# A hybrid decoder trunk: recurrent chains of two head pairs run side by side, and the output projection's order of contraction

## The chip, the cores and the metric

One core of one Trainium2 chip. The metric is the time of one execution on the device, in microseconds, as the median of several runs. Of one execution there is also a hardware trace. TensorE multiplies matrices (its weight loads are traced apart), VectorE, ScalarE and GpSimd (POOL) do the elementwise work, and SyncE (SP) issues the DMAs.

## The reference, cut to what matters

Two residual layers over 512 tokens of width 1024. Layer 0 mixes tokens by sparse attention, layer 1 by a recurrence (RWKV-7). Both add a cross-attention into 256 memory tokens, project the concatenated heads and end with a SwiGLU FFN. The recurrence of layer 1 has 12 heads of width 64; per head, step by step:

```python
def step(state, inp):
    r_t, w_t, k_t, v_t, a_t, b_t = inp
    sa = jnp.einsum('bhvk,bhk->bhv', state, a_t)
    state = state * w_t[:, :, None, :] + sa[..., None] * b_t[:, :, None, :] \
        + v_t[..., None] * k_t[:, :, None, :]
    return state, jnp.einsum('bhvk,bhk->bhv', state, r_t)
...
y = ((y - mean) * lax.rsqrt(var + GN_EPS)).reshape(B, S, MIX_WIDTH)
y = y * lnx_w.astype(jnp.float32) + lnx_b.astype(jnp.float32)
out = (y + bonus.reshape(B, S, MIX_WIDTH)) * g.astype(jnp.float32)
...
x = x + jnp.concatenate([mix, cross], axis=-1) @ w_o[i]
x = x + _swiglu(_rmsnorm(x, norm2[i]), w_ffn_in[i], w_ffn_out[i])
```

## The kernel before

All activations lie with features on the 128 partitions and the 512 tokens along the row. Large products are made of 128x128x512 matmuls of float32 operands that are split into a high and a low part, three matmuls for each (`mm3`, L686; `gemm`, L692; weights are loaded by `wraw`, L667, and split by ScalarE and VectorE in `wsplit`, L672).

The program is first recorded as a list of operations (`Rec`), and then a planner (`schedule`, L317) makes the order of each engine from estimated costs: the ready operation with the lowest number goes first. It may run ahead of the oldest operation not yet issued by a number of operations that depends on the kind (`LOOK`, L541: 600 for most, 1650 for the projections marked as filler), as far as buffers allow (84 shared row buffers `s2`, 8 PSUM banks, a share of both held back) and weights up to a quota (`QUOTA`, L520: 14 buffers, 24 in the phase named "ffn"). On TensorE it prefers an operation of the tile size that is running, within a limit of numbers (`TILED`, L528). What it lays down is fixed; on the chip each engine works through its list in order.

Layer 1 (`rwkv`, L1237): the projections of r, k and v by `gemm`, then for each of 6 pairs of heads `rwkv_pair` (L1336). It prepares decay, gates and keys with small low-rank products, among them the five matmuls of the gate, whose result ScalarE copies to the tile `dgt`. `rwkv_unit` (L1448) then turns the recurrence into 8 chunks of 64 tokens: matrices within a chunk (tiles `ar`, `bk`, `gram`, `tm`, and five levels of a triangular inverse in `tT`, `tQ`), all by 64x64 matmuls, one for each of the two heads, that sit in different corners of TensorE. This part is called the unit below. Its last loop is the chain: for every chunk, a right-hand side from the state (ScalarE copies it to `pad`), the solution u (copied by ScalarE again), the new state (VectorE, with a scaled old state from POOL), and an output of the chunk (`py`, copied to `ry`). After the chain the output is normalized, transposed (`gyo`), the bonus added and multiplied by the gate into `ot`. Pair m+1 follows pair m in the list, so the planner lays the unit of the next pair, and projections, between the steps of a chain. Every matmul of float32 operands of width 64 shows as two records in the trace.

The output projection (`out_proj`, L895) splits the eight tiles `ot` (`oxh`, `oxl`; 0 to 5 are mixer heads, 6 and 7 the memory's) and makes eight `gemm`s over all eight tiles in order, each with its bank, then adds the residual. In layer 0, heads come in four groups of three, and the compressed branch (`otc`) is added to tiles 0 to 5 after the last group.

Of the kernel before, what the change touches and what calls it, by code (L numbers as in the profile page):

```python
# [19 lines left out]
S = 512  # L20
# [218 lines left out]
class Rec:  # L239
# [16 lines left out]
    def add(self, eng, meth, args, kw, alts=()):  # L256
# [12 lines left out]
        if after is not None:  # L269
            dep(after, 0)  # L270
# [270 lines left out]
LOOK = {"far": 1650, "all": 600, "sync": 300, "w": 3000}  # L541
# [75 lines left out]
class B:  # L617
# [277 lines left out]
    def out_proj(self, i, ot, back):  # L895

        nc = self.nc
        xs = [self.split(ot[k], "ox") for k in range(KT)]
        xt = []
        for m in range(8):  # L900
            x = self.s2("xt")
            nc.sync.dma_start(x, back[m])
            ps = self.gemm(self.a[f"w_o{i}"][m], xs)
            nc.vector.tensor_tensor(out=x, in0=ps, in1=x, op=ALU.add)
            xt.append(x)
        return xt
# [37 lines left out]
    def nsa(self, xt):  # L944
# [215 lines left out]
        for g in range(G):  # L1160
# [15 lines left out]
            for qt in range(4):  # L1176
# [60 lines left out]
    def rwkv(self, xt):  # L1237
# [83 lines left out]
        pads = [self.s2("pad", F32, (128, 6, 64)) for _ in range(2)]  # L1321
        pad = [[t[:, j] for j in range(6)] for t in pads]
        for m in range(6):
            r, v = pair(m, m, "rr", 12 + m, 12 + m, "rv_")
            if m == RW_MEM[0]:
                kv = self.mem_kv(1)
            if m == RW_MEM[1]:
                qm = pair(21, None, "qm", 22, None, "qm")
            for j in range(2):
                if m == RW_MEM[2 + j]:  # L1330
                    ot[6 + j] = self.s2("ot")
                    self.mem_attn(j, qm[j], kv, ot)
            ot[m] = self.rwkv_pair(m, r, ks[m], v, rns, selT, zs, dv, pad[m % 2])
        return ot

    def rwkv_pair(self, m, r, k, v, rns, selT, zs, dv, pad):  # L1336
# [58 lines left out]
        wend = self.sm("wend", [128, 8], bufs=3)  # L1395
# [14 lines left out]
        Sp, Rp, Up = [pad[0], pad[1]], [pad[2], pad[3]], [pad[4], pad[5]]  # L1410
        nc.gpsimd.memset(Sp[0], 0.0)
        y = self.s2("ry")
        self.uev = None
        self.rwkv_unit(c3(r), c3(wc), c3(iw), c3(kn), c3(ka), c3(kp), vf, wend, Sp, Rp, Up, y)

        y3 = c3(y)
        mu = self.sm("gmu", [128, 8])
        nc.vector.tensor_reduce(out=mu, in_=y3, op=ALU.add, axis=AX.X)
        nc.vector.tensor_scalar(out=mu, in0=mu, scalar1=1.0 / 64, scalar2=None, op0=ALU.mult)
        tt(out=y3, in0=y3, in1=mu[:, :, None].to_broadcast([128, 8, 64]), op=ALU.subtract)  # L1420
        sq = self.s2("gsq")
        nc.scalar.activation(sq, y, AF.Square)
        var = self.sm("gvar", [128, 8])
        nc.vector.tensor_reduce(out=var, in_=c3(sq), op=ALU.add, axis=AX.X)
        nc.vector.tensor_scalar(out=var, in0=var, scalar1=1.0 / 64, scalar2=64e-5, op0=ALU.mult,
                                op1=ALU.add)
        rs = self.rsqrt(var, [128, 8], "gn")
        tt(out=y3, in0=y3, in1=rs[:, :, None].to_broadcast([128, 8, 64]), op=ALU.mult)

        yo = self.s2("gyo")  # L1430
        yo4 = yo.rearrange("p (b j t) -> p b j t", b=4, j=2)
        pt = self.ax_ps()
        for b in range(4):
            nc.tensor.transpose(pt[:, b * 128:b * 128 + 128], y[:, b * 128:b * 128 + 128],
                                self.ident)
        p4 = pt.rearrange("p (b i t) -> p b i t", b=4, i=2)
        for i in range(2):
            hs = slice(64 * i, 64 * i + 64)
            for j in range(2):
                nc.scalar.activation(yo4[hs, :, j, :], p4[64 * j:64 * j + 64, :, i, :],  # L1440
                                     AF.Identity, bias=self.v("lnb", m)[hs],
                                     scale=self.v("lnw", m)[hs])
        tt(out=yo, in0=yo, in1=bon, op=ALU.add)
        o = self.s2("ot")
        tt(out=o, in0=gt, in1=yo, op=ALU.mult)
        return o

    def rwkv_unit(self, r3, wc3, iw3, kn3, ka3, kp3, vf, wend, Sp, Rp, Up, y):  # L1448
# [107 lines left out]
        nc.scalar.copy(tfin, ps)  # L1556

        for cc in range(8):
            c = cc % 4
            ar, LR, MR = ars[cc // 4], LRB[cc // 4], MRK[cc // 4]  # L1560
            st, s_new = Sp[cc % 2], Sp[(cc + 1) % 2]
            rh, u = Rp[cc % 2], Up[cc % 2]
            vc = vf[:, cc]
            ps = self.ax_ps()[:, 0:64]
            both(ps, MR[:, c, 0], vc, True, False, after=self.uev)
            both(ps, ar[:, c, 0], st, False, True)
            rev = nc.scalar.copy(rh, ps)
            ps = self.ax_ps()[:, 0:64]
            both(ps, tfin[:, cc], rh, True, True)
            self.uev = nc.scalar.copy(u, ps)  # L1570
            if cc < 7:
                sw = self.sm("sw", [128, 64], bufs=3)
                wl = wend[:, cc:cc + 1]
                nc.gpsimd.tensor_scalar(out=sw, in0=st, scalar1=wl, scalar2=1.0,
                                        op0=ALU.mult, op1=ALU.mult)
                ps = self.ax_ps()[:, 0:64]
                both(ps, ktm[:, cc], vc, True, False, after=rev)
                both(ps, btm[:, cc], u, False, True)
                nc.vector.scalar_tensor_tensor(out=s_new, in0=ps, scalar=wl, in1=sw,
                                               op0=ALU.mult, op1=ALU.add)  # L1580
            ps = self.ax_ps("py")[:, 0:64]
            both(ps, ar[:, c, 1], st, True, False, after=rev)
            both(ps, MR[:, c, 1], vc, False, False)
            both(ps, LR[:, c, 1], u, False, True)
            nc.scalar.copy(y[:, cc * 64:cc * 64 + 64], ps)
# [177 lines left out]
```

## Time and profile before

| | us |
|---|---|
| median of 3 runs | 1470.31 |
| lowest, highest | 1467.98, 1472.65 |
| the profiled execution | 1467.86 |
| its span, first to last instruction | 1466.0 |
| TensorE busy | 1434.5 (98%) |
| VectorE busy | 870.5 (59%) |
| ScalarE busy | 689.5 (47%) |
| POOL busy | 121.8 (8%) |

A matmul's end in the trace is modelled, and matmuls overlap; what one costs is read from start to start. The trace has the stages in this order: layer 0's attention up to about 287 us, its output projection up to 335, the FFN up to 691, layer 1's first projections up to 763, the recurrence up to 1060, its output projection up to 1094, and the second FFN with the final norm.

### The profile page before, as it was taken

To read this page: it belongs to the slowest core of one execution; us is meant where nothing else is said; L and a number is where in the kernel's file an instruction comes from. 1 tells how busy PE (TensorE), PEld (TensorE's weight loads), DVE (VectorE), ACT (ScalarE), POOL (GpSimd) and SP (SyncE) were. 2 spreads that over 40 slices of the span, in tenths; PEclk is the share of its full clock that TensorE was granted. 3 is DMA by queue.
4 is the path that set the end of the run, shared out by engine and by line. 5 is a ranking of instruction groups with operands and counts; after the bars stand their busy time and mean duration, and the time that the engine had idled before them with its cause. 6 is when DMAs were issued, how large, how long until landed. Compare 5 with 4: busy or idle time off the path is not lost.

```text
span 1466.0 us, 25256 instructions
## 1 busy us (share of the span) xinstructions
PE 1434.5 (98%) x9914; PEld 1154.3 (79%) x9914; DVE 870.5 (59%) x1806; ACT 689.5 (47%) x1570; POOL 121.8 (8%) x217
## 2 busy tenths in 40 slices
PE   9999999999999999999999999998999999999997
PEld 7977777788888888888777777776678888888886
DVE  7785589974444534455569586787274444434435
ACT  7674578753313432233555575686363322312314
POOL 0231024300000000000000110120000000000003
PEclk9999999999999999999999999998999999999999
DMA  7324423142233322333221201101232332332212
GB/s 250 121 70 128 124 65 110 57 133 84 86 115 101 129 93 94 101 115 106 87 86 52 67 23 39 45 16 45 79 123 83 103 115 88 101 101 86 83 58 77
DMA packets 50232, 133.42 MB, mean 91 GB/s; under 512 B 6208, under 2 KB 14784, under 8 KB 50112
## 3 DMA queue, kind: packets, MB, share of 16 engines
q1 hardware_dynamic: 50112, 131.80, 28.4%
q8 instruction: 78, 1.28, 0.4%
q14 instruction: 42, 0.34, 0.1%
HBM read 122.34 MB, written 4.19 MB: 86 GB/s over the span
## 4 chain that ended last, share of the span: by engine, by line
PE 87%; DVE 6%; ACT 4%; issue 1%; DMA 1%; POOL 1%; SPq 0%; ACTq 0%; DVEq 0%; POOLq 0%
PE pm L516 68%; PE pa L516 13%; PE pv L516 2%; PE ptr L516 1%; PE po L516 1%; PE py L516 1%; ACT gyo L516 1%; POOL p L516 1%; ACT p L516 1%; DVE ot L516 1%; DVE gram L516 1%; DVE wsp L516 0%; DVE p L516 0%; DVE apl L516 0%; DMA kl<-kl 0%
## 5 line engine op out<-in xcount | busy, mean ns | idle before, releaser
L516 PE MATMUL pm<-fxh,wsp 128*128 128x512 f32 x1408 | 434.8, 389 | 0.0
L516 DVE TENSOR_TENSOR wsp<-wraw,wsp 128x512 fp32r<-128x512 f32 (+2 forms) x432 | 279.2, 659 | 51.3 <-ACT wsp L516 50.7
L516 PEld LDWEIGHTS pm<-fxh,wsp 128*128 128x128 f32 x1408 | 264.3, 188 | 55.0
L516 ACT CAST wsp<-wraw 128x512 fp32r<-128x512 f32 (+2 forms) x432 | 238.8, 592 | 96.8 <-DMA wraw<-w_fi 63.6
L516 PE MATMUL pm<-fxl,wsp 128*128 128x512 f32 x704 | 274.2, 389 | 0.0
L516 PE MATMUL pm<-hxh,wsp 128*128 128x512 f32 (+1 forms) x736 | 220.4, 380 | 0.0
L516 PEld LDWEIGHTS pm<-hxh,wsp 128*128 128x128 f32 x736 | 136.3, 188 | 26.3
L516 PEld LDWEIGHTS pm<-fxl,wsp 128*128 128x128 f32 x704 | 132.1, 188 | 27.2
L516 PE MATMUL pm<-hxl,wsp 128*128 128x512 f32 (+1 forms) x368 | 139.5, 380 | 0.0
L516 PE MATMUL pm<-wxh,wsp 128*128 128x512 f32 x368 | 130.7, 415 | 0.0
L516 DVE TENSOR_TENSOR xt<-pm,xt 128x512 f32<-128x512 f32 (+1 forms) x80 | 50.3, 636 | 130.5 <-PE pm L516 130.4
L516 ACT CAST hxh<-hu 128x512 fp32r<-128x512 f32 x44 | 27.3, 620 | 208.7 <-DVE hu L516 208.7
L516 DVE TENSOR_TENSOR hu<-pm,R 128x512 f32<-128x512 f32 x44 | 30.4, 692 | 120.7 <-PE pm L516 120.7
L516 ACT ACTIVATE hg<-hg 128x512 f32<-128x512 f32 x44 | 27.8, 632 | 153.2 <-DVE hg L516 153.2
L516 PE MATMUL pm<-oxh,wsp 128*128 128x512 f32 x256 | 86.3, 406 | 1.6 <-DVE wsp L516 0.7
L516 PE MATMUL pm<-nxh,wsp 128*128 128x512 f32 x256 | 86.3, 400 | 0.8 <-ACT nxh L516 0.8
L516 PEld LDWEIGHTS pm<-wxh,wsp 128*128 128x128 f32 x368 | 67.6, 188 | 19.1 <-issue 5.6
L516 PEld LDWEIGHTS pm<-hxl,wsp 128*128 128x128 f32 x368 | 69.2, 188 | 13.1
L516 DVE TENSOR_TENSOR hg<-pm,R 128x512 f32<-128x512 f32 x44 | 30.4, 691 | 79.6 <-PE pm L516 74.5
L516 POOL TENSOR_SCALAR p<-p,ars,gate 128x128 f32<-128x128 f32 (+3 forms) x96 | 63.1, 671 | 169.4 <-DVE ars L516 84.2
L516 PE MATMUL pm<-wxl,wsp 128*128 128x512 f32 x184 | 75.5, 410 | 0.0
L516 ACT ACTIVATE p<-p,amn 128x128 f32<-128x128 f32 (+3 forms) x96 | 53.4, 559 | 12.0 <-DVE amn L516 11.7
(317 smaller groups left out, 2284.1 us busy)
## 6 DMA issues: line engine op xcount, KB each, us to landing
wraw<-w_fi SPq DMA_DIRECT2D x88, 512.0 KB, 3.4
wraw<-w_fo SPq DMA_DIRECT2D x24, 512.0 KB, 3.4
wraw<-w_rw SPq DMA_DIRECT2D x23, 512.0 KB, 3.5
wraw<-w_fo SPq DMA_DIRECT2D x24, 384.0 KB, 3.0
wraw<-w_o SPq DMA_DIRECT2D x16, 512.0 KB, 3.5
wraw<-w_nsa SPq DMA_DIRECT2D x12, 512.0 KB, 3.8
xt<-xT SPq DMA_DIRECT2D x16, 256.0 KB, 3.8
bias<-bias SPq DMA_DIRECT2D x12, 256.0 KB, 3.9
```

The source lines that it names most:

```text
L516: o.ret = getattr(getattr(nc, o.eng), o.meth)(*[res(x) for x in o.args], **{k: res(v) for k, v in o.kw.items()})
```

## The change

The recurrence's chains are taken out of `rwkv_unit`. For each of three groups, two pairs are prepared (each with its unit), and then `rwkv_chain` runs both chains step by step: the matmuls of both pairs for one sum go to one PSUM bank, 64 columns each, and one ScalarE copy of 128 columns takes both. The state update is still one VectorE and one POOL operation for each pair. `rwkv_out` normalizes the outputs in two blocks of four chunks for both pairs, and makes the gate products only there, after the last u of the chain; the multiplication reads them from PSUM. `out_proj` goes through the eight output tiles in two halves of four: for each half first the contraction over the tiles 0 to 3, 6 and 7, then over 4 and 5; four banks are held meanwhile. It runs in the phase "ffn". In layer 0, `otc` is added to tiles 0 to 3 after the third group and to 4 and 5 after the fourth. The lookahead for most operations goes from 600 to 900, and the first part of the memory attention of layer 1 comes one pair earlier.

```diff
...
-LOOK = {"far": 1650, "all": 600, "sync": 300, "w": 3000}
+LOOK = {"far": 1650, "all": 900, "sync": 300, "w": 3000}
...
-    def out_proj(self, i, ot, back):
...
+    def out_proj(self, i, ot, back, late):
+        nc = self.nc
+        early = [k for k in range(KT) if k not in late]
+        xs = {k: self.split(ot[k], "ox") for k in early}
         xt = []
+        for m0, n in zip((0, MO[0]), MO):
+            ps, ws = [], []
+            for ks in (early, late):
+                for j in range(n):
+                    if ks is early:
+                        x = self.s2("xt")
+                        nc.sync.dma_start(x, back[m0 + j])
+                        xt.append(x)
+                        ws.append(self.wload(self.a[f"w_o{i}"][m0 + j]))
+                        ps.append(self.mm_ps())
+                    for k in ks:
+                        if k not in xs:
+                            xs[k] = self.split(ot[k], "ox")
+                        wh, wl = ws[j][k // 4]
+                        w = slice(k % 4 * 128, k % 4 * 128 + 128)
+                        self.mm3(ps[j], wh[:, w], wl[:, w], *xs[k], k == early[0], k == late[-1])
+                    if ks is late:
+                        x = xt[m0 + j]
+                        nc.vector.tensor_tensor(out=x, in0=ps[j], in1=x, op=ALU.add)
         return xt
...
+            for m in {2: (0, 1, 2, 3), 3: (4, 5)}.get(g, ()):
+                nc.vector.tensor_tensor(out=ot[m], in0=ot[m], in1=otc[m], op=ALU.add)
...
-        for m in range(6):
-            nc.vector.tensor_tensor(out=ot[m], in0=ot[m], in1=otc[m], op=ALU.add)
...
-            ot[m] = self.rwkv_pair(m, r, ks[m], v, rns, selT, zs, dv, pad[m % 2])
+        for g in range(3):
+            pairs = []
+            for m in (2 * g, 2 * g + 1):
+                r, v = pair(m, m, "rr", 12 + m, 12 + m, "rv_")
+                if m == RW_MEM[0]:
+                    kv = self.mem_kv(1)
+                if m == RW_MEM[1]:
+                    qm = pair(21, None, "qm", 22, None, "qm")
+                for j in range(2):
+                    if m == RW_MEM[2 + j]:
+                        ot[6 + j] = self.s2("ot")
+                        self.mem_attn(j, qm[j], kv, ot)
+                pairs.append(self.rwkv_pair(m, r, ks[m], v, rns, selT, zs, dv))
+            ys = self.rwkv_chain(pairs)
+            ot[2 * g], ot[2 * g + 1] = self.rwkv_out(2 * g, pairs, ys, zs)
...
-        ps = self.ax_ps()
-        self.mm3(ps, wh[:, 256:384], wl[:, 256:384], zgh, zgl, True, False)
-        nc.tensor.matmul(ps, wh[:, 384:512], z32, start=False, stop=False)
-        nc.tensor.matmul(ps, wl[:, 384:512], z32, start=False, stop=True)
-        gt = self.s2("dgt")
-        nc.scalar.copy(gt, ps)
...
+    def rwkv_out(self, m0, pairs, ys, zs):
...
+        for j in range(2):
+            wh, wl = pairs[j]["wg"]
+            tt(out=yos[j], in0=yos[j], in1=pairs[j]["bon"], op=ALU.add)
+            ps = self.ax_ps("pg")
+            nc.tensor.matmul(ps, wh[:, 256:384], zgh, start=True, stop=False, after=self.uev)
+            nc.tensor.matmul(ps, wh[:, 256:384], zgl, start=False, stop=False)
+            nc.tensor.matmul(ps, wl[:, 256:384], zgh, start=False, stop=False)
+            nc.tensor.matmul(ps, wh[:, 384:512], z32, start=False, stop=False)
+            nc.tensor.matmul(ps, wl[:, 384:512], z32, start=False, stop=True)
+            o = self.s2("ot")
+            tt(out=o, in0=ps, in1=yos[j], op=ALU.mult)
+            out.append(o)
+        return out
...
+    def rwkv_chain(self, pairs):
+        nc = self.nc
+        heads = [slice(64 * i, 64 * i + 64) for i in range(2)]
+        def sums(name, *terms, after=None):
+            ps = self.ax_ps(name)[:, 0:128].rearrange("p (j d) -> p j d", j=2)
+            first = [None, None]
+            for n, (w, x) in enumerate(terms):
+                for j in range(2):
+                    for i, hs in enumerate(heads):
+                        o = nc.tensor.matmul(ps[hs, j], w(j)[hs], x(j)[hs],
+                                             start=n == 0 and j == 0, stop=n == len(terms) - 1,
+                                             tile_position=(64 * i, 64 * i), skip_group_check=True,
+                                             after=[first[i]] if first[i] else
+                                             [after] if after else None)
+                        first[i] = first[i] or o
+            return ps
+        S = self.sm("cS", [128, 2, 64], bufs=3)
+        nc.gpsimd.memset(S, 0.0)
+        ys = [self.s2("ry", F32, (128, 4, 2, 64)) for _ in range(2)]
+        uev = None
         for cc in range(8):
+            q, c = cc // 4, cc % 4
+            al = lambda j: pairs[j]["ars"][q][:, c, 0]
+            rho = lambda j: pairs[j]["ars"][q][:, c, 1]
+            rbt = lambda j: pairs[j]["LRB"][q][:, c, 1]
+            mt = lambda j: pairs[j]["MRK"][q][:, c, 0]
+            rkt = lambda j: pairs[j]["MRK"][q][:, c, 1]
+            tf, bt, kt, v = (lambda j, n=n: pairs[j][n][:, cc] for n in ("tfin", "btm", "ktm", "vt"))
+            st = lambda j, S=S: S[:, j]
+            ps = sums("pa", (mt, v), (al, st), after=uev)
+            rh, u = self.sm("crh", [128, 2, 64], bufs=2), self.sm("cu", [128, 2, 64], bufs=2)
             rev = nc.scalar.copy(rh, ps)
+            ps = sums("pa", (tf, lambda j: rh[:, j]))
+            uev = nc.scalar.copy(u, ps)
+            ut = lambda j: u[:, j]
             if cc < 7:
+                sw = self.sm("sw", [128, 2, 64], bufs=2)
+                for j in range(2):
+                    nc.gpsimd.tensor_scalar(out=sw[:, j], in0=S[:, j],
+                                            scalar1=pairs[j]["wend"][:, cc:cc + 1], scalar2=1.0,
+                                            op0=ALU.mult, op1=ALU.mult)
+                ps = sums("pa", (kt, v), (bt, ut), after=rev)
+                S = self.sm("cS", [128, 2, 64], bufs=3)
+                for j in range(2):
+                    nc.vector.scalar_tensor_tensor(out=S[:, j], in0=ps[:, j],
+                                                   scalar=pairs[j]["wend"][:, cc:cc + 1],
+                                                   in1=sw[:, j], op0=ALU.mult, op1=ALU.add)
+            ps = sums("py", (rho, st), (rkt, v), (rbt, ut), after=rev)
+            nc.scalar.copy(ys[q][:, c], ps)
+        self.uev = uev
+        return ys
...
-            xt = self.out_proj(i, ot, back)
+            nc.phase = "ffn"
+            xt = self.out_proj(i, ot, back, [[4, 5], [4, 5]][i])
...
-RW_MEM = [0, 4, 5, 5]
+RW_MEM = [0, 4, 4, 5]
+MO = [4, 4]
```

## Rows read from the trace of the kernel before

**Rows 1.** Page, part 1: busy us, share of the span, instructions of each engine.
```profile
PE 1434.5 (98%) x9914; PEld 1154.3 (79%) x9914; DVE 870.5 (59%) x1806; ACT 689.5 (47%) x1570; POOL 121.8 (8%) x217
```

**Rows 2.** Stretches: from:to us, engines' busy us (instructions), granted clock, DMA share, GB/s.
```profile
335.00:691.00 356.00, 356.00 (x1573) 294.77 (x1572) 169.58 (x279) 113.34 (x209) 2.35 (x6) 1.00 0.32 102
...
763.00:1023.00 260.00, 250.95 (x3992) 185.72 (x3991) 200.21 (x443) 173.36 (x439) 32.42 (x62) 0.98 0.15 46
1023.00:1060.00 37.00, 37.00 (x458) 24.02 (x457) 10.26 (x21) 10.82 (x35) 2.28 (x6) 0.96 0.21 73
```

**Rows 3.** Timeline, TensorE, one chunk of the last chain: start us, us, instruction.
```profile
1038.30 0.33 PE L516 MATMUL pa<-pad,tfin 64*64 64x64 f32 x4
...
1038.91 0.51 PE L516 MATMUL pm<-oxl,wsp 128*128 128x512 f32 x1
1039.34 0.33 PE L516 MATMUL pa<-pad,tm 64*64 64x64 f32 x4
...
1039.84 0.73 PE L516 MATMUL pm<-oxh,wsp 128*128 128x512 f32 x2
1040.50 0.33 PE L516 MATMUL pa<-pad,ar 64*64 64x64 f32 x4
1040.76 0.51 PE L516 MATMUL pm<-oxl,wsp 128*128 128x512 f32 x1
...
1041.43 0.33 PE L516 MATMUL pa<-pad,tfin 64*64 64x64 f32 x4
```

**Rows 4.** Timeline, TensorE: the first and the last of the stretches counted.
```profile
774.62 1.10 PE L516 MATMUL pa<-ar,bk 64*64 64x128 f32 x32
...
1058.19 0.33 PE L516 MATMUL py<-pad,gram 64*64 64x64 f32 x4
```

**Rows 5.** Critical chain, one piece: start us, us, what.
```profile
287.27 43.13 PE pm L516 x190
```

**Rows 6.** Groups by operation: shapes, count | busy us, mean ns | idle before, releasers.
```profile
L516 DVE TENSOR_TENSOR hu<-pm,R 128x512 f32<-128x512 f32 x44 | 30.4, 692 | 120.7 <-PE pm L516 120.7
...
L516 ACT COPY pad<-pa 128x64 f32<-128x64 f32 x96 | 20.4, 215 | 38.8 <-PE pa L516 38.2
...
L516 ACT COPY tm<-pa 64x256 f32<-64x256 f32 x46 | 16.8, 366 | 7.8 <-PE pa L516 6.7 <-DVE tm L516 0.5
...
L516 DVE SCALAR_TENSOR_TENSOR pad<-pa,wend,sw 128x64 f32<-128x64 f32 x42 | 11.9, 283 | 39.0 <-PE pa L516 36.3 <-PE py L516 2.2 <-POOL sw L516 0.2
...
L516 ACT COPY ry<-py 128x64 f32<-128x64 f32 x48 | 10.3, 215 | 21.5 <-PE py L516 21.2
...
L516 DVE TENSOR_TENSOR ot<-dgt,gyo 128x512 f32<-128x512 f32 x6 | 4.1, 690 | 0.2
...
L516 ACT COPY dgt<-pa 128x512 f32<-128x512 f32 x6 | 3.6, 593 | 0.0
```

**Rows 7.** Stretches, finer, all engines.
```profile
200.00:220.00 20.00, 17.84 (x92) 13.01 (x91) 19.46 (x62) 17.57 (x54) 7.33 (x10) 1.00 0.13 41
...
273.00:287.00 14.00, 12.40 (x68) 9.75 (x67) 13.90 (x33) 9.79 (x24) 4.88 (x6) 1.00 0.01 2
...
763.00:806.00 43.00, 42.51 (x619) 32.32 (x617) 39.72 (x92) 26.75 (x60) 3.12 (x3) 1.00 0.25 75
...
1007.00:1026.00 19.00, 13.56 (x213) 10.03 (x213) 13.58 (x28) 13.69 (x27) 0.00 (x0) 0.64 0.17 57
...
1058.00:1070.00 12.00, 10.83 (x50) 8.20 (x50) 7.68 (x16) 6.09 (x12) 0.00 (x0) 1.00 0.12 45
```

**Rows 8.** Timeline, TensorE, the last pair's unit: idle before in brackets.
```profile
1017.97 0.44 PE L516 MATMUL pa<-tT,lth 64*64 64x64 f16 x16 [2.06 <-ACT tT L516]
...
1019.10 0.80 PE L516 MATMUL pm<-oxh,wsp 128*128 128x512 f32 x1 [0.43 <-ACT oxh L516]
```

**Rows 9.** Timeline, TensorE and VectorE, at the end of the last chain.
```profile
1069.28 0.96 PE L516 MATMUL pm<-oxh,wsp 128*128 128x512 f32 x3 [0.68 <-DVE wsp L516]
...
1069.31 0.69 DVE L516 TENSOR_TENSOR oxl<-ot,oxh 128x512 fp32r<-128x512 f32 x1
```

More of the change, by code (lines that the diff above doesn't have):

```diff
@@ L268, in add @@
         after = kw.pop("after", None)
-        if after is not None:
-            dep(after, 0)
+        for o in after if isinstance(after, list) else [after]:
+            if o is not None:
+                dep(o, 0)
         for v in ins:
@@ L892, in mem_attn @@
                                     op=ALU.add)
-    def out_proj(self, i, ot, back):
+    def out_proj(self, i, ot, back, late):
         nc = self.nc
-        xs = [self.split(ot[k], "ox") for k in range(KT)]
+        early = [k for k in range(KT) if k not in late]
+        xs = {k: self.split(ot[k], "ox") for k in early}
         xt = []
[L900 to L905, printed above, removed]
+        for m0, n in zip((0, MO[0]), MO):
[17 more added lines that the diff above has]
+                        nc.vector.tensor_tensor(out=x, in0=ps[j], in1=x, op=ALU.add)
         return xt
@@ L1320, in rwkv, with rwkv_pair @@
         ot = [None] * 8
[L1321 to L1332, printed above, removed]
-            ot[m] = self.rwkv_pair(m, r, ks[m], v, rns, selT, zs, dv, pad[m % 2])
+        for g in range(3):
[13 more added lines that the diff above has]
+            ot[2 * g], ot[2 * g + 1] = self.rwkv_out(2 * g, pairs, ys, zs)
         return ot
-    def rwkv_pair(self, m, r, k, v, rns, selT, zs, dv, pad):
+    def rwkv_pair(self, m, r, k, v, rns, selT, zs, dv):
         nc = self.nc
@@ L1409, in rwkv_pair @@
         vf = vt
[L1410 to L1428, printed above, removed]
@@ L1443, in rwkv_pair @@
[L1443 to L1448, printed above, removed]
+        c = self.rwkv_unit(c3(r), c3(wc), c3(iw), c3(kn), c3(ka), c3(kp))
+        c.update(vt=vt, wend=wend, bon=bon, wg=(wh, wl))
+        return c
+    def rwkv_out(self, m0, pairs, ys, zs):
+        nc = self.nc
+        tt = nc.vector.tensor_tensor
+        zw, za, zgh, zgl, z32 = zs
+        yos = [self.s2("gyo") for _ in range(2)]
+        for q, y in enumerate(ys):
+            yf = y.rearrange("p c j d -> p (c j d)")
+            y3 = y.rearrange("p c j d -> p (c j) d")
+            mu = self.sm("gmu", [128, 8])
+            nc.vector.tensor_reduce(out=mu, in_=y3, op=ALU.add, axis=AX.X)
+            nc.vector.tensor_scalar(out=mu, in0=mu, scalar1=1.0 / 64, scalar2=None, op0=ALU.mult)
+            tt(out=y3, in0=y3, in1=mu[:, :, None].to_broadcast([128, 8, 64]), op=ALU.subtract)
+            sq = self.s2("gsq")
+            nc.scalar.activation(sq, yf, AF.Square)
+            var = self.sm("gvar", [128, 8])
+            nc.vector.tensor_reduce(out=var, in_=sq.rearrange("p (c d) -> p c d", c=8), op=ALU.add,
+                                    axis=AX.X)
+            nc.vector.tensor_scalar(out=var, in0=var, scalar1=1.0 / 64, scalar2=64e-5,
+                                    op0=ALU.mult, op1=ALU.add)
+            rs = self.rsqrt(var, [128, 8], "gn")
+            tt(out=y3, in0=y3, in1=rs[:, :, None].to_broadcast([128, 8, 64]), op=ALU.mult)
+            pt = self.ax_ps()
+            for c in range(4):
+                nc.tensor.transpose(pt[:, c * 128:c * 128 + 128],
+                                    y[:, c].rearrange("p j d -> p (j d)"), self.ident)
+            p4 = pt.rearrange("p (c i t) -> p c i t", c=4, i=2)
+            for j in range(2):
+                for i in range(2):
+                    hs = slice(64 * i, 64 * i + 64)
+                    nc.scalar.activation(
+                        yos[j][hs, 256 * q:256 * q + 256].rearrange("p (c t) -> p c t", c=4),
+                        p4[64 * j:64 * j + 64, :, i, :], AF.Identity,
+                        bias=self.v("lnb", m0 + j)[hs], scale=self.v("lnw", m0 + j)[hs])
+        out = []
+        for j in range(2):
[11 more added lines that the diff above has]
+        return out
@@ L1450, in rwkv_unit @@
+    def rwkv_unit(self, r3, wc3, iw3, kn3, ka3, kp3):
         nc = self.nc
@@ L1556, in rwkv_unit @@
         nc.scalar.copy(tfin, ps)
-        for cc in range(8):
[L1559 to L1566, printed above, removed]
+        return dict(ars=ars, LRB=LRB, MRK=MRK, btm=btm, ktm=ktm, tfin=tfin)
@@ L1567, in rwkv_unit @@
             rev = nc.scalar.copy(rh, ps)
-            ps = self.ax_ps()[:, 0:64]
-            both(ps, tfin[:, cc], rh, True, True)
-            self.uev = nc.scalar.copy(u, ps)
+            ps = sums("pa", (tf, lambda j: rh[:, j]))
+            uev = nc.scalar.copy(u, ps)
+            ut = lambda j: u[:, j]
             if cc < 7:
[L1572 to L1585, printed above, removed]
+                sw = self.sm("sw", [128, 2, 64], bufs=2)
[3 more added lines that the diff above has]
+                                            op0=ALU.mult, op1=ALU.mult)
```

14 lines of the change are left out of this document (1 added, 13 removed).

## The prediction

> **What bounds it now.** I read the page's busy shares first: TensorE is busy for 1434.5 of 1466.0 us [rows 1], so only what shortens TensorE's own sequence counts. The stretches come next. The first FFN (335 to 691) is one unbroken row of 512-column matmuls, TensorE busy for all 356 us [rows 2]; a like row of 190 on the critical chain takes 43.13 us, 0.227 us each [rows 5]. Nothing the change does can shorten that. The RWKV stretch (763 to 1060) is different: also almost always busy, but with some 4450 short matmuls [rows 2]. There "busy" hides a cost that only the timeline shows.
>
> That cost is the change between 64x64 matmuls (chains, and the units that prepare them) and full 128x128 ones. Start to start in one chunk of the last chain [rows 3]: a stretch of 4 small records lasts 0.26 us (1040.50 to 1040.76), of 12 0.50 us, of 16 0.61 us. The slope is (0.61-0.26)/12 = 0.029 us a record, and 0.26 - 4x0.029 = 0.14 us is left however long the stretch is. A single full matmul between two such stretches takes 0.43 us (1038.91 to 1039.34), two take 0.66, where 0.227 each is their bare price: 0.20 us more per visit. One trip there and back costs 0.14+0.20 = 0.34 us. Counting in the timeline the small stretches with full matmuls on both sides, from the one at 774.62 to the one at 1058.19 [rows 4], gives 175: 88 of chain matmuls alone, 54 of unit matmuls alone, 33 mixed. 175x0.34 = 60 us of a 284 us stretch are switches.
>
> **The paired chains.** Each pair's chain has 8 chunks of 3 dependent steps (right-hand side, u, state), 6x8x3 = 144 steps, which stand in 88+33 = 121 stretches. Side by side, two pairs take one step together: 72 steps. The matmuls themselves stay (their records included), so 0.029 us each is unchanged. By the old share 72 steps fill 72x121/144 = 60 stretches, of which half the 33 mixed ones, 16, carry unit matmuls too; the other 17 pieces of unit work come to stand alone, 54+17 = 71. New count 60+71 = 131, so 44 trips fewer: 44x0.34 = 15.0 us. Bounds: if no unit matmul shares a stretch with a chain any more, 72 + (54+33) = 159, saving 16 trips, 5.4 us; if the unit's own stretches don't grow, 60+54 = 114, saving 61, 20.7 us. I take 15, from the old share.
>
> The length of a chain does not enter while TensorE has other work, but its pressure does. A chunk takes 1041.43-1038.30 = 3.13 us [rows 3]. Side by side each of three steps has 4 more records before its reader starts (3x0.117), two ScalarE copies are twice as wide (0.215 us for 64 columns, 0.366 for 256 [rows 6]: about 0.05 more each), and a second VectorE update of 0.283 follows the first: 3.13+0.35+0.10+0.28 = 3.86 us. A chain is 31 us, three are 93 us, against 6x25 = 150 us now.
> Today's copy starts after all matmuls of its bank. The Trainium skill (PSUM — Partial Sum Buffer, PSUM bank collisions raise a hardware error) says that a reader must be kept off a bank that TensorE writes, even at other columns, which speaks against sharing one: the first pair's copy must wait for the second pair's matmuls. No row of this trace shows a bank with two pairs. Without that wait the chunk would be some 0.35 us shorter, and no term of the sum changes except the uncovered end.
>
> ScalarE loses work: 144 copies (96 and 48) become 72, and the six gate copies of 0.593 us go [rows 6]. It is off the path (173 of 260 us busy in 763 to 1023 [rows 2]): 0 us. If its cover went, each chain step would feel it, which the 3.86 us has in. POOL and VectorE keep their 42 scalings and 42 updates.
>
> **Gate products behind the chain.** The same five matmuls a pair, ten of 0.227 us (2.3 us) in the last group, move from the pair's preparation to after its last u. The product then reads PSUM instead of a copy; a VectorE multiplication with a PSUM operand costs 0.692 against 0.690 [rows 6]. Two more weight tiles a pair are held until then. At the end of the stage these matmuls fall where TensorE waits for tiles anyway (0.68 us idle before 1069.28 [rows 9]): 0 us, at most +2.3 if that wait is gone.
>
> **Output projection of layer 1, lookahead, quota.** Today the last chain matmul starts at 1058.19 [rows 4] and the split of the last tile ends at about 1070 [rows 9], 11 to 12 us filled by projection matmuls of the first five tiles (50 TensorE instructions in 1058 to 1070 [rows 7]). The sore place is earlier: 1007 to 1026, the last pair's unit, with TensorE busy 13.56 of 19 us at a mean granted clock of 0.64 [rows 7], between its 1.2 and 2.4 GHz levels, after waits of 0.43 to 2.06 us for VectorE and ScalarE [rows 8]. Bare work in it is about 7 us and switches 1 us, so some 9 us are lost. Projection matmuls arrive only at 1019.10 [rows 8], because the lookahead of 600 operations ends before them.
> The new order offers 4x6x3 = 72 early matmuls at once, and 18 for each tile of the second half that finds a bank; of 8 banks the first half holds 4, and chain and products need 2 or 3, so one or two: 90 to 108. Demand: the last chain leaves 31 us less its own small work (8 chunks x 64 records x 0.029 = 15 us, 24 trips = 8 us), 8 us or 34 matmuls; its tail now has two pairs, two more VectorE operations of 0.69 after the normalization, 1.4 us longer, 13 us or 55 matmuls less the products' 10: 45. Total 79, leaving 11 to 29 for the unit, 2.5 to 6.6 us. I take the low end, -2.5, against +1.4 for the longer tail: -1 us. Bounds: -6.6 if all is well placed; +7 if the unit eats the early matmuls and the tail stands open. The banks' reserve decides. The weight quota of 24 costs nothing by itself: it lets four tiles' weights (16 buffers) stand, which 14 would not.
>
> **Layer 0.** Early matmuls of heads 0 to 7 may fill TensorE's idle at the end of the attention: 2.2 us in 200 to 220, 1.6 us in 273 to 287. But VectorE is busy 19.46 of 20 and 13.90 of 14 us there [rows 7], and each early tile and weight needs a VectorE split, of about 0.69 us. I take 0, bounds -6 and +3. The two FFNs: 0, their row of matmuls is gapless.
>
> **A cost of waiting for two units.** The first chain now waits for two units, in a stretch where VectorE is already at 39.72 of 43 us [rows 7]. Projections of later pairs cover TensorE; bounds 0 and +5, I take +1.
>
> **Sum.** -15 -1 +0 +1 = -15 us. The profiled execution took 1467.86 us, with a span of 1466.0; that gives 1452.9. The median of the three runs is 2.45 us above it: 1455.
>
> **Rivals.**
> *A, larger gain.* The wider lookahead also fills the last unit's stall and the attention's end: -20.7 -6.6 -3 = -30 us, 1440. For: both holes are plain in the rows. Against: VectorE's load, and the few free banks.
> *B, no net gain.* Switches fall by only 16 trips (-5.4) and the opened tail costs +5: within 2 us, 1470. For: unit work may lose its companion stretches. Also here: the planner counts each switch as less than the 0.34 us measured and may go on visiting full matmuls one by one.
> *C, slower: VectorE becomes the bound between the chains.* Now each chain runs over the next pair's unit. Two pairs' intermediate tiles (some 13 of the 84 shared buffers a pair) could keep the next unit from starting under a chain. Then chains and unit work add up. VectorE is busy 200.2+10.3 us in 763 to 1060 [rows 2]; less 12 for state updates and 25 for outputs (six of 0.69 a pair [rows 6]), 173 us of unit work. At 0.92 density [rows 7] that is 188, plus 93 for chains and 8 for outputs not covered: 289 us, against 295 now to the last chain matmul: still not slower. It decides at a density of 173/194 = 0.89; the stretch as a whole has 200.2/260 = 0.77 [rows 2], with today's overlap. At 0.85 it is 305 us, +10: 1480. TensorE then waits between chains and drops to its lower clock as in 1007 to 1026.
> The Trainium skill (TensorE: Matmul & The Clock Gate, Part 1) has the lower clock as the idle default; the 0.64 in [rows 7] agrees.
> Against C: free slots under a chain go to the lowest waiting number, which is unit work, and the projections' weights take few buffers.
>
> **Chances.** Forecast 0.58 (own range 1445 to 1465), A 0.14, B 0.12, C 0.16. A difference under 0.3% (4.4 us) is what a measurement here cannot tell from none. Faster: 0.57 of the forecast and A, 0.71; same: B and the forecast's edge, 0.13; slower: 0.16. The range leaves out the outer half of C and the far end of A: 1438 to 1476.
>
> **What would show it.** Right: some 115 to 145 small stretches where 175 were; chunk periods near 3.9 us and three chains; projection matmuls before 1007; FFNs unchanged at 0.227 us. Wrong: stretches above 155; TensorE idle between chains with VectorE above 0.9 (C); a gap after the last chain with ScalarE or VectorE ending it; a clock below 1 elsewhere.

## The result, and the profile after

The change makes the kernel 1.0% faster: 1455.55 us (median of 4 runs, 1455.09 to 1458.44) against 1471.42 us (median of 4, 1467.98 to 1472.65) on the same chip, ratio 0.990 with a 95% interval of 0.9878 to 0.9922. The profiled execution took 1455.25 us, span 1453.5; before it took 1467.86, span 1466.0: 12.6 us less in these two, where the medians are 15.9 apart. The stages below are read from these two executions.

Page, part 1, of the kernel after; it answers to [rows 1]:

```profile
PE 1414.3 (97%) x9914; PEld 1154.0 (79%) x9914; DVE 875.7 (60%) x1819; ACT 676.1 (47%) x1479; POOL 123.2 (8%) x214
```

The TensorE instructions are the same 9914; what fell by 20 us is the time in which it counts as busy. Where it fell is read from the stretches (columns as in [rows 2]):

```profile
335.00:691.00 356.00, 356.00 (x1576) 294.99 (x1575) 169.72 (x284) 112.14 (x207) 2.71 (x7) 1.00 0.32 104
763.00:1020.00 257.00, 247.03 (x4059) 189.47 (x4059) 209.23 (x455) 160.40 (x359) 25.30 (x54) 1.00 0.18 55
980.00:1007.00 27.00, 23.61 (x375) 17.36 (x375) 23.62 (x41) 17.15 (x36) 0.00 (x0) 1.00 0.23 68
1007.00:1047.00 40.00, 39.78 (x635) 29.47 (x634) 13.16 (x34) 15.53 (x40) 3.65 (x12) 1.00 0.33 106
1046.00:1062.00 16.00, 11.90 (x49) 9.29 (x46) 9.98 (x20) 6.63 (x13) 0.00 (x0) 0.89 0.21 66
```

The first FFN is gapless as before. The old hole at the last pair's unit, 1007 to 1026 (5.44 us idle, clock 0.64, [rows 7]), has shrunk and moved. After, TensorE is idle 3.39 us in 980 to 1007, at clock 1.00, mostly in front of these two steps of the last unit:

```profile
986.26 1.10 PE L517 MATMUL pa<-dbon,hbr 128*128 128x512 f32 x2 [1.26 <-ACT oxh L517]
...
993.26 0.65 PE L517 MATMUL pa<-chh,lth 64*64 64x64 f16 x16 [1.50 <-DVE lth L517]
```

From 1007 to 1047 it is busy 39.78 of 40 us. A new hole stands behind the last chain, at 1046 to 1062: busy 11.90 of 16 us.

In these two executions all of the gain lies in one stage. From the first `pm<-wxh` to the last `pm<-oxh` of layer 1 it was 401.4 us (687.7 to 1089.1) and is 386.6 (689.7 to 1076.3): -14.8. What lies ahead is 2.0 us longer, what follows 0.3.

I split this stage into three parts for every kernel below. *Bare*: its matmuls at the cadence they have in an unbroken row (0.227 us for 512 columns [rows 5], 0.029 us a 64x64 record [rows 3], other shapes at theirs). I estimate 328.8 us; the matmuls are the same in every kernel, so it falls out of every difference. *Switches*: the number of small stretches, counted as in [rows 4], times 0.335 us (between the forecast's 0.34 and what E1 gives below). *Standing*: the rest, waits and matmuls at the half clock. Before: 175 stretches, 58.6 us, and 14.0 standing. After: 121 stretches, 40.5 us, and 17.4 standing.

Standing is a remainder and moves with the price: at the 0.367 us of the probes below it would go from 8.4 to 13.4. The trace has a count of its own, TensorE's waits over 0.15 us in the stage without what the clock costs: 10.0 us before and 13.9 after, 4.2 in E1, 19.9 in E2, 13.3 in E5, 7.0 in E9, 19.7 in E3, 14.3 in E13.

One chunk of the last chain in the timeline of TensorE after, to be held against [rows 3]:

```profile
1026.19 0.45 PE L517 MATMUL pa<-crh,tfin 64*64 64x64 f32 x8
1026.47 0.40 PE L517 MATMUL pa<-vt,tm 64*64 64x64 f32 x8
...
1028.02 0.50 PE L517 MATMUL pm<-oxh,wsp 128*128 128x512 f32 x1
1028.45 0.45 PE L517 MATMUL pa<-cS,ar 64*64 64x64 f32 x8
1028.83 0.50 PE L517 MATMUL pm<-oxl,wsp 128*128 128x512 f32 x1
1029.16 0.62 PE L517 MATMUL pm<-oxh,wsp 128*128 128x512 f32 x2
1029.72 0.45 PE L517 MATMUL pa<-crh,tfin 64*64 64x64 f32 x8
```

Eight records stand where four stood, and their stretch lasts 0.38 us (1028.45 to 1028.83) where four took 0.26: the four added cost 0.12 us, their bare price. From 1026.19 to 1028.02 one small stretch holds what stood in two, those at 1038.30 and 1039.34 in [rows 3]: this chunk of two pairs has two stretches, one of a single pair had three. It takes 3.53 us, where a single pair's took 3.13.

The groups of operations after (columns as in [rows 6]):

```profile
L517 POOL TENSOR_SCALAR sw<-cS,wend 128x64 f32<-128x64 f32 x42 | 15.4, 380 | 334.8 <-DVE wend L517 178.8 <-DVE cS L517 155.8
...
L517 DVE SCALAR_TENSOR_TENSOR cS<-pa,wend,sw 128x64 f32<-128x64 f32 x42 | 10.1, 279 | 22.6 <-PE pa L517 22.5
...
L517 ACT COPY crh<-pa 128x128 f32<-128x128 f32 x24 | 6.4, 265 | 10.9 <-PE pa L517 10.7
L517 ACT COPY ry<-py 128x128 f32<-128x128 f32 x24 | 6.4, 265 | 14.2 <-PE py L517 14.0
L517 ACT COPY cu<-pa 128x128 f32<-128x128 f32 x24 | 6.4, 265 | 13.5 <-PE pa L517 13.2
```

144 ScalarE copies of 215 ns became 72 of 265 ns. The tail, TensorE:

```profile
1049.55 0.39 PE L517 MATMUL pm<-oxh,wsp 128*128 128x512 f32 x1
1051.65 0.63 PE L517 MATMUL pa<-cf,ry 128*128 128x128 f32 x4 [1.72 <-DVE ry L517]
1054.67 0.50 PE L517 MATMUL pg<-zgxh,wsp 128*128 128x512 f32 x1 [2.39 <-ACT gyo L517]
```

The early projection matmuls run out at 1049.55. TensorE waits 1.72 us for the normalization, does four matmuls, and stands 2.39 us more: the second pair's gate product comes when ScalarE's `gyo` is done (I take it that it needs a bank which `gyo` reads; that was not separated). From 1055.3 the granted clock is 0.5 for 3.4 us.

### The profile page after: what moved, and what is told of

The parts are those of the page before. It is cut to its first block, busy times and chain, and to the rows that moved or that the text cites. A ratio compares the mean times of both kernels' runs of the same rounds, so it can differ in the third digit from the quotient of the medians.

```text
span 1453.5 us, 25111 instructions
## 1 busy us (share of the span) xinstructions
PE 1414.3 (97%) x9914; PEld 1154.0 (79%) x9914; DVE 875.7 (60%) x1819; ACT 676.1 (47%) x1479; POOL 123.2 (8%) x214
## 4 chain that ended last, share of the span: by engine, by line
PE 73%; DVE 3%; ACT 3%; issue 1%; POOL 0%; ACTq 0%; POOLq 0%; DVEq 0%
PE pm L517 63%; PE pa L517 8%; PE py L517 1%; DVE gram L517 1%; ACT gyo L517 1%; PE pg L517 1%; ACT tm L517 1%; POOL p L517 0%; ACT L517 0%; DVE tm L517 0%; ACT vt L517 0%; ACT wsp L517 0%; DVE dbon L517 0%; DVE zd L517 0%; DVE lth L517 0%
## 5 line engine op out<-in xcount | busy, mean ns | idle before, releaser
L517 PE MATMUL pm<-wxh,wsp 128*128 128x512 f32 x368 | 126.5, 407 | 0.5 <-DVE wsp L517 0.5
L517 ACT ACTIVATE hg<-hg 128x512 f32<-128x512 f32 x44 | 27.9, 634 | 153.1 <-DVE hg L517 153.1
L517 PE MATMUL pm<-nxh,wsp 128*128 128x512 f32 x256 | 89.9, 412 | 1.1 <-ACT nxh L517 1.1
L517 POOL TENSOR_SCALAR p<-p,ars,gate 128x128 f32<-128x128 f32 (+3 forms) x96 | 67.5, 717 | 175.9 <-DVE ars L517 88.0
```

The source lines that it names most:

```text
L517: o.ret = getattr(getattr(nc, o.eng), o.meth)(*[res(x) for x in o.args], **{k: res(v) for k, v in o.kw.items()})
```

## The experiments

**P1, P2: what does a switch cost?** Both add the same work to the kernel before: 88 pairs of 64x64 matmuls into a bank that nothing reads, 44 in each of the two FFNs, rows without gaps. `e7_probe_single` puts one pair behind each of the 88 products, `e7_probe_batched` puts eight (at the end four) behind every eighth.

```diff
...
                 ps = self.gemm(W[j], xs)
+                trips += 1
+                probe(1)   # batched: probe(8) at every eighth, probe(4) at 44
...
```

> The kernel before, with 88 small stretches put into the two gapless FFNs, one after every second-half and first-half product: each is one pair of 64x64 float32 matmuls (4 records) into a bank that nobody reads. Switch theory: each visit costs 0.26 us for the stretch and 0.20 us at the full matmuls, 0.46 us, so 88x0.46 = +40 us, about 1511. Rival, that the residue in the recurrence is waiting for ScalarE and VectorE and not the change of tile size: only the matmuls' own 0.117 us, +10 us, about 1481.

> The same 88 pairs of small matmuls, but eight (at the end of an FFN four) in a row, 12 stretches instead of 88. Switch theory: 352 records x 0.029 = 10 us and 12 x 0.34 = 4 us, +14 us, about 1485; the difference to the kernel with single pairs is 76x0.34 = 26 us. Rival: as with single pairs, difference 0.

Measured: 1512.8 us (1511.83 to 1513.18; ratio 1.0279, 1.0264 to 1.0294) and 1484.92 us (1482.52 to 1485.48; 1.0092, 1.0075 to 1.0109), beside 1471.21 before. The same 88 pairs in 12 stretches and not in 88 save 27.9 us: 27.9/76 = 0.367 us a trip. One trip in the timeline of the single probe:

```profile
348.53 0.39 PE L516 MATMUL pm<-fxl,wsp 128*128 128x512 f32 x1
348.76 0.39 PE L516 MATMUL pm<-fxh,wsp 128*128 128x512 f32 x1
349.07 0.33 PE L516 MATMUL px<-cf 64*64 64x64 f32 x4
349.34 0.50 PE L516 MATMUL pm<-fxh,wsp 128*128 128x512 f32 x1
349.67 0.39 PE L516 MATMUL pm<-fxl,wsp 128*128 128x512 f32 x1
```

The last full matmul ahead holds 0.31 us, not 0.227; the four records 0.27, not 0.117; the first full one behind 0.33. That is 0.34 us lost at one trip where nothing waits for anything. The Trainium skill (TensorEngine Tiling (Array Packing), Key Properties) says that a change of tiling mode drains TensorE; these rows, with 0.34 us lost, fit that and give the price.

**E1, E2: the two halves of the change alone.** `e1_order_only` takes the kernel before with the new output projection, the lookahead of 900, layer 0's earlier additions and the memory attention's new place; the chains stay single and the gate products early. `e2_chains_only` takes the paired chains with the gate products behind them, with the old projection and 600.

```diff
...
-            xt = self.out_proj(i, ot, back)
+            xt = self.out_proj(i, ot, back, [[4, 5], [4, 5]][i])   # e1 only
...
-            ot[m] = self.rwkv_pair(m, r, ks[m], v, rns, selT, zs, dv, pad[m % 2])
+            ys = self.rwkv_chain(pairs)   # e2 only
...
```

> Only the second half of the change: the projection's order in halves with tiles 4 and 5 last, lookahead 900, quota, the earlier additions in layer 0, the earlier memory attention; chains one by one and gate products as before. The order laid down has 182 small stretches (175 before). Switch theory: +2 us for 7 more, less a few us of the last unit's stall, 1463 to 1472. Rival, that the gain is the filled stall and the projection: about 1456.

> Only the first half: paired chains in shared banks and gate products behind the chain; projection, lookahead 600, quota, layer 0 and memory attention as before. 108 small stretches. Switch theory: 67 fewer, -23 us, less what stands open because the early projection is missing under the last unit, chain and tail (3 to 12 us): 1450 to 1460. Rival, that the projection's order makes the gain: about 1471.

Measured: E1 1461.0 us (1459.77 to 1462.47; 0.9928, 0.9913 to 0.9944), E2 1464.09 us (1463.25 to 1467.2; 0.9953, 0.9936 to 0.9970). Both lie outside what was expected for them: E1 below its 1463 to 1472, E2 above its 1450 to 1460, and neither at its rival's number. In the stage: E1 393.0 us, -8.4; E2 395.3 us, -6.1. Together -14.5, where the whole change has -14.8: the halves add up. (E2's profiled execution, 1467.2 us, was the slowest of its four; the others are within 1463.25 to 1464.89.)

How each comes by its part differs. E1 has 182 stretches, seven more than before, but 3.3 us standing where there were 14.0: the new order fills the last unit. Its stage takes 64.2 us beyond the bare cadences, and the trace shows TensorE waiting 4.2 us of them; the other 60.0 us on 182 stretches are 0.33 us each, the switch price once more. This figure rests on the estimate of the bare part, as the probes' does not. E2 has 108 stretches, 67 fewer, worth 22 us, but 30.3 us standing: 16 of the 22 us are lost again. TensorE of E2, the stretch of the last unit and the tail:

```profile
987.83 1.10 PE L517 MATMUL pa<-dbon,hbr 128*128 128x512 f32 x2 [2.37 <-DVE dbon L517]
995.38 0.65 PE L517 MATMUL pa<-chh,lth 64*64 64x64 f16 x16 [3.10 <-DVE lth L517]
...
1051.40 1.09 PE L517 MATMUL pa<-cf,ry 128*128 128x128 f32 x4 [3.53 <-DVE ry L517]
1054.87 0.79 PE L517 MATMUL pm<-oxh,wsp 128*128 128x512 f32 x1 [2.38 <-ACT gyo L517]
```

The last unit waits for VectorE and the tail for the normalization, with nothing to put between, and both stretches are at a reduced clock (0.83 in 980 to 1010, 0.79 in 1046 to 1070).

**E3, E13: the lookahead.** `e3_look600` is the kernel after with 600; `e13_before_look900` is the kernel before with 900 and nothing else.

```diff
...
-LOOK = {"far": 1650, "all": 900, "sync": 300, "w": 3000}
+LOOK = {"far": 1650, "all": 600, "sync": 300, "w": 3000}
...
```

> The changed kernel with the lookahead back at 600 and all else as changed. 121 small stretches, as with 900. If the reach of the lookahead is what brings projection matmuls under the last unit, the standing time there comes back: 1459 to 1464. If the new order of the projection does it without the reach: 1455 to 1457.

> The kernel before with nothing but the lookahead at 900. 186 small stretches (175 before): +3.7 us. If the reach alone fills the last unit's stall, as in the kernel with only the order's part: 1460 to 1465. If the reach needs the projection's new order to have ready matmuls to reach for (every tile of it waits at tiles 4 and 5 with few banks): 1468 to 1476.

Measured: E3 1466.68 us (1465.99 to 1471.31; 0.9975, 0.9964 to 0.9987), 11 us above after; E13 1476.95 us (1476.13 to 1478.03; 1.0042, 1.0027 to 1.0058), 5.4 us slower than before (stage 407.7 us, 186 stretches, 16.6 standing). E3 lies above both ranges expected for it, E13 1 us above its second. With the old order the reach costs time, and without the reach the new order, on top of E2, gives none. E3 keeps 121 stretches and has 29.3 us standing, 12 more than after (read in an execution of 1471.31 us, the slowest of its ten, so it may be some us high); its last unit:

```profile
992.05 2.07 PE L517 MATMUL pa<-dbon,hbr 128*128 128x512 f32 x2 [2.25 <-DVE dbon L517]
1000.86 0.76 PE L517 MATMUL pa<-chh,lth 64*64 64x64 f16 x16 [3.90 <-DVE lth L517]
```

And the tail of E13, after the last chain matmul:

```profile
1063.64 0.28 PE L516 MATMUL py<-pad,gram 64*64 64x64 f32 x4
1069.43 1.09 PE L516 MATMUL pa<-cf,ry 128*128 128x128 f32 x4 [5.51 <-DVE ry L516]
1074.98 2.08 PE L516 MATMUL pm<-oxh,wsp 128*128 128x512 f32 x4 [4.47 <-ACT oxh L516]
```

Counting layer 1's 192 projection matmuls by place goes far to explain it. Before: 24 run ahead of the last chain, 43 under it, 35 in its tail. E13: 65, 40 and none. After: 51, 41 and 16. The stock that can run before the last tiles are ready is 102, 105 and 108: hardly moved. With the old order the reach only lets the planner spend it sooner; E13 fills the unit (no wait there is over 0.4 us any more) and pays with 10 us of open tail at a clock of 0.70 (1058 to 1080). In other kernels the stock does move: of the 192, those that start before the last `ot` is made are 103, 105 and 109 in these three, but 142 in E1, 122 in E5, 93 in E3 and 63 in E2.

**E4: the shared bank.** `e4_own_banks` gives each pair its own bank and copy.

```diff
...
-            ps = self.ax_ps(name)[:, 0:128].rearrange("p (j d) -> p j d", j=2)
+            pj = [self.ax_ps(name)[:, 0:64] for _ in range(2)]
...
```

> The changed kernel, with the two pairs still in step, but each pair's sum in a bank of its own and copied by ScalarE on its own (144 copies of 64 columns again, not 72 of 128). 123 small stretches, 121 with the change. Switch theory: the shared bank and the halved copies are not where the gain comes from: 1454 to 1459. Rival, that fewer ScalarE instructions make the gain: most of the 16 us goes, 1464 or more.

Measured: 1455.76 us (1453.56 to 1455.85; 0.9897, 0.9881 to 0.9914): as after. The last chain's chunks, from one `tfin` step to the next, take 3.49 us on average (1014.3 to 1038.7, seven) against 4.00 in after (1015.2 to 1043.2). The chain is shorter by half a microsecond a chunk, and the total does not move: while TensorE has other work, the chain's length does not enter. Sharing the bank is not where the gain comes from.

**E5, E8: gate products back in the preparation.** `e5_gate_early` has the old five matmuls and the copy; `e8_replan` is E5 with the planner's price of a switch at 170 and the lookahead at 1000.

```diff
...
+        gt = self.s2("dgt")
+        nc.scalar.copy(gt, ps)
...
-            tt(out=o, in0=ps, in1=yos[j], op=ALU.mult)
+            tt(out=o, in0=pairs[j]["gt"], in1=yos[j], op=ALU.mult)
...
-                            o.end += 97
+                            o.end += 170   # e8 only
...
```

> The changed kernel with the gate products back in each pair's preparation and copied by ScalarE. 116 small stretches, 121 with the change. Switch theory: 5 fewer, -1.7 us; and the wait of 2.39 us of the last products at the end of the chain for a bank goes: 1449 to 1454. Rival, that the products behind the chain are filler which the tail needs: the tail stands open longer, 1457 or more.

> The kernel with early gate products, and the planner told a price of 170 ns in place of 97 for each change of tile size, and a lookahead of 1000. 111 small stretches, 121 with the change: -3.4 us, and no wait of the products: 1446 to 1453. If the standing time grows with the longer lookahead, as much as is saved: 1455.

Measured: E5 1457.38 us (1455.18 to 1458.91; 0.9912, 0.9897 to 0.9927), E8 1454.78 us (1452.96 to 1457.88; 0.9898, 0.9881 to 0.9914). Both missed what I expected first (1449 to 1454, 1446 to 1453), the time that an open tail won would give. The tail was won: 25 projection matmuls follow the last chain matmul before the normalization is through, where after has 16, and TensorE of E5 is busy 25.74 of 26 us there (1052 to 1078). But E5 has 20.0 us standing in the stage, more than after, now at the unit:

```profile
991.89 1.10 PE L517 MATMUL pa<-dbon,hbr 128*128 128x512 f32 x2 [2.60 <-DVE dbon L517]
...
1000.51 0.44 PE L517 MATMUL pa<-tT,lth 64*64 64x64 f16 x16 [0.89 <-DVE tT L517]
1002.05 0.64 PE L517 MATMUL pa<-tQ,tT 64*64 64x64 f16 x16 [1.10 <-DVE tQ L517]
```

The products' place moves the hole, not the time. E8 cut the stretches to 111, and 19.2 us stood; its time is that of its other branch, 1455, in which the standing eats what the switches save.

**E9, E11: the last two pairs alone.** Pairs 0 to 3 go in twos, 4 and 5 one after the other as before. `e11_alone_replan` is E9 with the gate products early for all, the price 170 and a stronger preference of the planner for staying in a mode (200 for 100).

```diff
...
+                if g in (2,):
+                    ot[m] = self.rwkv_pair1(m, r, ks[m], v, rns, selT, zs, dv, pad[m % 2])
+                    continue
...
-TILED = (800, 100)
+TILED = (800, 200)   # e11 only
...
```

> The changed kernel, but the last two pairs (4 and 5) run as before the change: each its unit, chain, output and early gate products, one after the other; pairs 0 to 3 in twos. 146 small stretches, 121 with the change: +25, +8.4 us. If the standing time that the change added (some 13 us in the recurrence and its tail) lies in the last group, 6 to 10 us of it go: 1452 to 1459. If it lies in all groups alike, 2 to 4 us go: 1460 to 1463.

> The last two pairs alone as in the kernel before, the gate products early for all pairs, the planner told 170 ns for a change of tile size and to prefer the running tile size a little longer (limit 200 in place of 100 on the full size). 137 small stretches, 121 with the change (+5.4 us); if the standing time stays as small as with the last two alone (about 10 us less than with the change): 1449 to 1453. If it grows as fast as stretches fall: 1455.

Measured: E9 1454.58 us (1450.82 to 1455.63; 0.9889, 0.9872 to 0.9906), E11 1457.74 us (1456.62 to 1459.53; 0.9909, 0.9894 to 0.9924). E9 has 146 stretches, 25 more than after (8.4 us), and 7.5 us standing, 9.9 less, within what was expected if the standing of after lies in the last group: more than half of it does. That it stands there because no further pair's projections are left to fill in is my reading and was not tested; E9 also makes the gate products of these two pairs early. The two stretches of E9 that answer to after's holes:

```profile
980.00:1010.00 30.00, 29.68 (x476) 20.72 (x475) 26.61 (x53) 18.14 (x53) 3.95 (x6) 1.00 0.13 41
...
1046.00:1070.00 24.00, 23.55 (x119) 18.65 (x119) 15.51 (x29) 13.77 (x27) 0.00 (x0) 1.00 0.07 23
```

E11 was to have both, few stretches and little standing; it has 137 and 13.7 us. It missed both ranges expected (1449 to 1453, or 1455).

**E12: own banks, memory attention earlier.** `e12_banks_mem` is E4 with the price 170 and the memory attention's steps at the pairs 0, 2, 3 and 4, to keep more single matmuls beside the early units.

```diff
...
-RW_MEM = [0, 4, 4, 5]
+RW_MEM = [0, 2, 3, 4]
...
```

> Pairs in step with a bank and a copy of its own for each, memory attention earlier (before pairs 2, 3 and 4 in place of 4, 4 and 5), the planner told 170 ns for a change of tile size. 124 small stretches, 121 with the change (+1 us). If the standing time before the last unit is for want of filler there, moving the memory attention forward does not help: 1455 to 1459; if it only shifts with the plan, 1451 to 1455.

Measured: 1457.26 us (1453.49 to 1459.21; 0.9902, 0.9879 to 0.9924), 124 stretches, 16.4 us standing: no gain. The time lies in the first of the two ranges expected (1455 to 1459, if filler is what is wanting under the last unit), but its runs reach into the second. None of the variants is below the kernel after by more than the intervals allow; the best, E9 and E8, are within 1 us of it.

## Why the prediction was right

The forecast was 1455, faster; measured was 1455.55. That it is so close is in part luck: two terms that were both off cancel, 3 us more saved in switches and 3.4 us more standing.

**The switch price: right.** 0.34 us was read from one chunk; the probes give 0.367 and E1 0.33. (Of the 4450 matmuls that the prediction calls short some 660 are not 64x64 ones; the stretches were counted among the 3792 that are.)

**The number of switches: right in kind, short in size.** Forecast 131 stretches, measured 121: 54 fewer, not 44, so -18 us (-20 at the probes' price), not -15, inside the bounds of 114 and 159. The step that was short is the share-out: I had 60 stretches with chain matmuls and 71 of unit matmuls alone. There are 35 of chain alone, 20 mixed and 66 of unit alone, so 55 and 66: the steps of a paired chain keep together more than single ones did.

**The chunk: right.** Forecast 3.86 us; 4.00 on average in the last chain. Without the shared bank I had it some 0.35 us shorter, and E4 has 0.51. That the chain's length does not enter the total, E4 shows.

**Last unit and tail: the net was small as forecast, the pieces were not.** I had -2.5 for the unit and +1.4 for the tail. At the unit 5.44 us of idle at a clock of 0.64 became 3.39 us at 1.00, more than -2.5 is worth; and the tail opened: 1.72 and 2.39 us of waiting, then half clock. (The prediction's "some 9 us" lost at the unit are 11 by its own figures, 19 less 7 and 1; no term is made of them.) The stock of early matmuls was forecast at 90 to 108 and is 108, and the last chain took 41 where I had 34. But the step that shares out the rest failed: I let the chain and the tail be served first, 79 of them, and gave the unit what remained, 11 to 29. The order served who came first: 51 went ahead of the last chain and 16 were left for the tail, of 45 wanted. That is rival B's opened tail; its other half, few trips saved, did not come. Over the stage, standing went from 14.0 to 17.4 us: +3.4, where my terms come to 0.

**What the two halves are.** The -1 of the forecast for order and reach was far too small: alone with the old chains they are worth 8.4 us in the stage (E1), since they clear 10.7 us of standing. The +1 for a first chain that waits for two units was about right. Its second step, the first that needs `tfin`, starts at 820.2 us where it started at 806.1, and around it TensorE is idle 2.29 us after and 0.49 before:

```profile
763.00:825.00 62.00, 61.51 (x1057) 46.75 (x1055) 49.42 (x111) 37.48 (x93) 5.68 (x10) 1.00 0.22 66
...
763.00:825.00 62.00, 59.71 (x849) 45.09 (x848) 54.83 (x125) 36.71 (x80) 3.06 (x4) 1.00 0.23 72
...
812.03 0.31 PE L517 MATMUL pa<-chh,lth 64*64 64x64 f16 x8 [1.17 <-DVE lth L517]
```

What the forecast had no term for is what the paired chains cost with the old order: 16 us more standing (E2), most of it not at the first chain but at the last unit (24.16 of 30 us busy in 980 to 1010) and in the tail (18.09 of 24 in 1046 to 1070), both at a reduced clock. With the reach cut back after has 12 us more of it (E3). So a large gain and a large loss, neither of them forecast, nearly cancel: in the whole change the two come out at +3.4.

**Gate products: 0, at most +2.3.** The wait of 2.39 us in front of the second product is not of their making alone: E2, with both products done, stands 2.38 us at the same step in front of a projection matmul. And E5, which has them early and no gap in the tail, is not faster. The 0 stands.

**Layer 0: 0.** It is 2.0 us longer after, but no evidence of a cost: the last `pm<-oxh` of layer 0 was at 326.6 us before, and at 331.1 in E2, 329.6 and 327.2 in the probes, all with the same order of layer 0's instructions; and at 328.6, 325.7, 329.7, 329.6 and 328.3 in after, E1, E4, E5 and E9, which share the other order. The means are 328.6 and 328.4. Part of the scatter comes from the start, where in some executions TensorE still runs its first projection matmuls at the lower of its two clock levels: the granted clock rises to 1.00 at 5.4 us before and at 10.8 after. These two stand at the same place, before and after:

```profile
7.16 0.39 PE L516 MATMUL pm<-nxl,wsp 128*128 128x512 f32 x1
...
8.28 0.63 PE L517 MATMUL pm<-nxl,wsp 128*128 128x512 f32 x1
```

E2, the single probe, E4 and E9 start like after, the batched probe, E1 and E5 like before. So the profile of before had the quicker start, and the 12.6 us between the two profiles may be short for that reason.

**The rivals.** C, VectorE as the bound between chains, fell: chains and units still overlap. VectorE is busy 209.23 of 257 us in 763 to 1020, 0.81, so one after the other they would have ended later than C's 305 us, at 1068 or behind; the last small matmuls start at 1045.64. A holds in part (the old hole smaller and at full clock, switches down by 54), but its 30 us were not reached, because standing came up elsewhere. Among the kernels with the new order and a reach of 900 or 1000, the standing is larger where the stretches are fewer: 3.3 us at 182 (E1), 7.5 at 146 (E9), 13.7 at 137 (E11), 16.4 and 14.4 at 124 and 123 (E12, E4), 17.4 at 121, 20.0 and 19.2 at 116 and 111 (E5, E8). E3 and E13 do not fit in: the same 121 stretches with 29.3 us, and 186 with 16.6. Why the others line up so I can only argue: fewer trips mean fewer places at which other matmuls fill a dependent step's wait, and the stock that could fill them is limited. It was not separated from the planner's own choices.

## What to carry to other kernels

Count the changes between matmul tile sizes in the timeline and price one trip with a probe in a gapless row: here 0.33 to 0.37 us, some 58 us of a 401 us stage, all of it counted as busy. Work that is ready early is a limited stock (that banks limit it was not tested): reaching further can spend it sooner and open the next gap (E13), unless the order itself makes more of it ready at the right place (E1). Test the halves of a change separately: here the new order covered most of the idle time that the paired chains bring alone, and a sum that is right can have wrong terms.

## What the chip showed that I had not expected

Eight 64x64 records between full matmuls cost just what the four-record slope said (0.38 against 0.26 + 0.12 us), so in these rows the price of a trip does not depend on its length. In layer 0, the same order of instructions ended up to 4.5 us apart between profiled executions (326.6 and 331.1): one profile alone can't carry a term of that size. Idle time was paid twice here: in after, 4.1 us of waiting behind the last chain are followed by 3.4 us at the half clock; in E3 3.90 us of idle at the unit stand beside a stretch at 0.72 (980 to 1010).
